# Seven products for every feature pair of both feed-forwards, with two of them made early on one token half, and 24 modulation columns moved into the mixing

## The chip, the cores and the metric

One core of a Trainium2 chip runs the whole program. The metric is device time in microseconds; lower is better. The kernel before takes 2085.41 us, the median of three runs (2083.35 to 2086.26).

## The reference

One layer over 1024 latent tokens and 256 context tokens of width 1024: feed-forward, token mixing, feed-forward, each behind a norm that is modulated by vectors computed from a condition, and a last norm.

```python
m_l = jnp.split(cond_lat @ ada_w[i] + ada_b[i], N_MOD, axis=-1)
x = x + 0.5 * m_l[2][:, None, :] * swiglu(modulate(rms_norm(x, norm1_w[i]), m_l[0], m_l[1]),
                                            ffn1_w1[i], ffn1_w3[i], ffn1_w2[i])
...
x = x + m_l[5][:, None, :] * y_l
x = x + 0.5 * m_l[8][:, None, :] * swiglu(modulate(rms_norm(x, norm3_w[i]), m_l[6], m_l[7]),
                                            ffn2_w1[i], ffn2_w3[i], ffn2_w2[i])
...
def swiglu(h, w1, w3, w2):
    return (jax.nn.silu(h @ w1) * (h @ w3)) @ w2
```

The context goes through the first feed-forward and the mixing with the same weights. `w1` and `w3` are 1024 x 2816, that is 22 features of 128 columns. The nine modulation vectors (0 to 8) have 8 columns of 128 numbers each.

## The kernel before, in words

Tensors lie with features on the partitions, tokens on the free axis, in two token halves of 512 (`tg` 0 and 1). Each f32 factor is split into a high and a low part (`hi` by a copy on ScalarE, `lo` by a subtraction on VectorE), and each product is three matmuls, hi hi, hi lo and lo hi (`mm3`, L426 to L428). A weight of one feature is 128 x 1024, loaded as two raw halves of 128 x 512 (`raw_half`, L659, a ring of NR = 6 tiles) and split into a ring of NH = 6 pairs (`half`, L666). All DMA goes through SyncE's (SP's) queue, in order.

**The hidden layer.** The classic way for two features is 2 features x 2 token halves x 8 blocks of 128 inputs, three matmuls each. `chain` (L699) does two features f and f + 1 in seven products instead, a scheme of Strassen's kind: `seven_w` (L679) makes seven combinations of the four quarters of the two weights (w1 to w7; w1 is the first half a11 of feature f, w2 its second half a12), and each is multiplied by a combination of four blocks of the input: b11 and b21 are the two halves of the inputs on token half 0, b22 the second on token half 1, and t1 to t4 are differences (the T blocks, made by `t_make`, L1101, or by `norm_t`, L633, and `t34_raw`). Each of the seven is four blocks deep, 12 matmuls. Sums of products are copied out of PSUM by ScalarE (`keep`), added by VectorE (`plus`) or accumulated in PSUM. `c_silu` and `c_mul` (L741) make silu(h w1) (h w3), and `g_out` (L749) makes the combinations of it that the back half uses and stores them in DRAM (`gd`). `hidden` (L816) runs `chain` for w1 and w3 of every pair, with `w2_sums` (L785) and some modulation columns (`mods`, up to MPER sums a call) between.

**The starts.** `chain` needs both token halves and the T blocks. So that TensorE has work before, features 0 to 3 of the first feed-forward and 0 and 1 of the second are done the classic way: `first1` (L1167) runs six weights of token half 0 block by block while the norm and its modulation columns are computed and token half 1 is loaded; `first2` (L1145) does the four weights of features 0 and 1 for token half 0, then 1. A dependency by hand (HELD) puts the last norm's diagonal matmuls (`rstd_rows`) behind the first seven blocks of `first2`.

**The columns.** A modulation column is one reduction on VectorE of 128 x 1024 products (`mod_sum`, L519; in halves of 512 in `mods_half`, L528). Ten come from small matmuls in `first1`, the others are spread over the first feed-forward (vectors 5, 2, 1, 0, 4, 3, 7, 6 in the order of EMODS), vector 8 over the second.

**Order.** `first1` is written in the order in which TensorE, VectorE and ScalarE run it. The feed-forwards are ordered by a scheduler that takes priorities from the program's order; loads and splits of weights are raised by 150 (WPRI). From the end of the first feed-forward to the start of the second a `Recorder` (L166) collects all operations, plans them with costs per engine and fixes the order of every engine; nearly all its instructions have the line L147. The mixing's tiles of 128 x 512 (`t`) come from a ring of NT2 = 5.

The first feed-forward's hidden layer runs to about 440 us, its back half and the context's to 850, the mixing to 1433, the second feed-forward to the end.

## Time and profile before

| | us |
|---|---|
| median of three runs | 2085.41 |
| the profiled execution | 2088.82 |
| its span, first to last instruction | 2087.0 |
| TensorE busy | 2071.6 (99%) |
| VectorE busy | 1471.9 (71%) |
| ScalarE busy | 973.3 (47%) |
| GpSimd busy | 199.3 (10%) |

The granted TensorE clock is 0.998 over the span, and the DMA engines moved 178 GB/s on average. On a page, `psa<-hh,whi` is a matmul that writes the PSUM tile psa from the moving operand hh and the weight whi; `x14` is a count; what stands in brackets behind a row of the timeline is the idle time before it and who ended it. PEld is the load of the stationary operand, which overlaps the matmuls.

### The profile page before, as it was taken

To read this page: it belongs to the slowest core of one execution; us is meant where nothing else is said; L and a number is where in the kernel's file an instruction comes from. 1 tells how busy PE (TensorE), PEld (TensorE's weight loads), DVE (VectorE), ACT (ScalarE), POOL (GpSimd) and SP (SyncE) were. 2 spreads that over 40 slices of the span, in tenths; PEclk is the share of its full clock that TensorE was granted. 3 is DMA by queue.
4 is the path that set the end of the run, shared out by engine and by line. 5 is a ranking of instruction groups with operands and counts; after the bars stand their busy time and mean duration, and the time that the engine had idled before them with its cause. 6 is when DMAs were issued, how large, how long until landed. Compare 5 with 4: busy or idle time off the path is not lost.

```text
span 2087.0 us, 34162 instructions
## 1 busy us (share of the span) xinstructions
PE 2071.6 (99%) x12352; PEld 1763.0 (84%) x12352; DVE 1471.9 (71%) x2660; ACT 973.3 (47%) x1818; POOL 199.3 (10%) x195
## 2 busy tenths in 40 slices
PE   9999999999999999999999999999999999999998
PEld 6888888888889999998788988888888888888888
DVE  6889999666776445765577478767776666765586
ACT  5433433435544445566475246444434344344553
POOL 0000000000015665001021001000000000010000
PEclk9999999999999999999999999999999999999999
DMA  9277667449886553674233233242344444477774
GB/s 348 84 241 237 232 217 256 149 165 371 277 289 222 181 183 115 195 219 129 76 108 98 79 91 105 90 162 81 112 156 147 144 163 157 151 235 229 218 237 151
DMA packets 201082, 370.58 MB, mean 178 GB/s; under 512 B 23249, under 2 KB 35921, under 8 KB 200785
## 3 DMA queue, kind: packets, MB, share of 16 engines
q1 hardware_dynamic: 200768, 368.33, 53.7%
q8 instruction: 97, 1.59, 0.3%
q14 instruction: 73, 0.59, 0.1%
q10 hardware_dynamic: 144, 0.07, 0.0%
HBM read 292.68 MB, written 67.24 MB: 172 GB/s over the span
## 4 chain that ended last, share of the span: by engine, by line
PE 77%; DVE 10%; DMA 8%; issue 3%; ACT 1%; SPq 0%; DVEq 0%; POOLq 0%; ACTq 0%
PE psa L147 18%; PE psa L426 10%; PE psa L428 10%; PE psa L427 10%; PE psb L147 9%; PE psb L427 7%; PE psb L428 7%; PE psb L426 7%; DVE junk L523 2%; DVE wlo L422 2%; DMA raw<-in_w 2%; DMA raw<-sd 2%; DVE hl L422 1%; DMA raw<-gd 1%; DMA hl<-sd 1%
## 5 line engine op out<-in xcount | busy, mean ns | idle before, releaser
L421 ACT ACTIVATE whi<-raw 128x512 fp32r<-128x512 f32 x371 | 233.9, 631 | 502.7 <-issue 160.6
L422 DVE TENSOR_TENSOR wlo<-raw,whi 128x512 fp32r<-128x512 f32 x371 | 254.1, 687 | 178.0 <-ACT whi L421 175.6
L426 PE MATMUL psa<-hh,whi 128*128 128x512 f32 x684 | 267.0, 390 | 1.2 <-ACT s L738 0.6
L428 PE MATMUL psa<-hh,wlo 128*128 128x512 f32 x684 | 266.3, 389 | 0.0
L427 PE MATMUL psa<-hl,whi 128*128 128x512 f32 x684 | 266.2, 389 | 0.0
L427 PE MATMUL psb<-hl,whi 128*128 128x512 f32 x568 | 221.6, 390 | 0.5 <-DVE hl L422 0.3
L428 PE MATMUL psb<-hh,wlo 128*128 128x512 f32 x568 | 221.3, 390 | 0.2 <-DVE wlo L422 0.2
L426 PE MATMUL psb<-hh,whi 128*128 128x512 f32 x568 | 221.1, 389 | 0.0
L426 PEld LDWEIGHTS psa<-hh,whi 128*128 128x128 f32 x684 | 128.4, 188 | 28.9 <-ACT s L711 1.7
L147 DVE TENSOR_TENSOR wlo<-raw,whi 128x512 fp32r<-128x512 f32 (+1 forms) x140 | 88.5, 647 | 90.8 <-ACT whi L147 80.1
L147 PE MATMUL psa<-hl,whi 128*128 128x512 f32 x384 | 152.5, 397 | 0.0
L147 PE MATMUL psa<-hh,whi 128*128 128x512 f32 x384 | 152.3, 397 | 0.0
L147 PE MATMUL psa<-hh,wlo 128*128 128x512 f32 x384 | 152.2, 396 | 0.0
L428 PEld LDWEIGHTS psa<-hh,wlo 128*128 128x128 f32 x684 | 128.4, 188 | 26.6
L427 PEld LDWEIGHTS psa<-hl,whi 128*128 128x128 f32 x684 | 128.5, 188 | 26.3
L422 POOL TENSOR_TENSOR hl<-s,hh 128x512 fp32r<-128x512 f32 x88 | 132.4, 1530 | 145.2 <-DVE hl L422 81.1
L147 ACT ACTIVATE whi<-raw 128x512 fp32r<-128x512 f32 (+1 forms) x140 | 82.5, 599 | 119.7 <-PE psa L147 94.1
L427 PEld LDWEIGHTS psb<-hl,whi 128*128 128x128 f32 x568 | 106.6, 188 | 24.7 <-DVE hl L422 2.7
L428 PEld LDWEIGHTS psb<-hh,wlo 128*128 128x128 f32 x568 | 106.6, 188 | 23.1 <-DVE wlo L422 1.2
L426 PEld LDWEIGHTS psb<-hh,whi 128*128 128x128 f32 x568 | 106.6, 188 | 22.2
L428 PE MATMUL psa<-hh,hl 128*128 128x256 f32 x392 | 111.1, 284 | 0.0
L426 PE MATMUL psa<-hh,hh 128*128 128x256 f32 x392 | 111.1, 283 | 0.0
(443 smaller groups left out, 4820.4 us busy)
## 6 DMA issues: line engine op xcount, KB each, us to landing
raw<-in_w SPq DMA_DIRECT2D x242, 256.0 KB, 3.3
s<-in_w SPq DMA_DIRECT2D x198, 256.0 KB, 3.7
gd<-s SPq DMA_DIRECT2D x154, 256.0 KB, 2.8
ada<-in_adaT SPq DMA_DIRECT2D x60, 512.0 KB, 4.6
raw<-gd SPq DMA_DIRECT2D x91, 256.0 KB, 3.5
sd<-s SPq DMA_DIRECT2D x44, 256.0 KB, 2.7
raw<-sd SPq DMA_DIRECT2D x44, 256.0 KB, 3.2
hh<-in_w SPq DMA_DIRECT2D x44, 256.0 KB, 4.0
```

Source lines behind the costliest of these rows:

```text
L147: self.rec.add(self.eng, lambda: f(*map(get, a), **{x: get(v) for x, v in k.items()}), outs, ins, name, a, k)
L421: nc.scalar.activation(hi, src, AF.Copy)
L422: (eng or nc.vector).tensor_tensor(out=lo, in0=src, in1=hi.bitcast(F32), op=ALU.subtract)
L426: mm(ps, wa[0], xa[0], start=start, stop=False, skip_group_check=more)
L427: mm(ps, wa[0], xa[1], start=False, stop=False, skip_group_check=more)
L428: return mm(ps, wa[1], xa[0], start=False, stop=stop, skip_group_check=more)
L523: nc.vector.tensor_tensor_reduce(out=self.junk, in0=t, in1=self.cs[s], scale=1.0, scalar=self.col("ada_b")[:, j:j + 1], op0=ALU.mult, op1= ...
```

## The change

Every pair of features now goes by seven products.

- For 8 of the 11 pairs of the first feed-forward (PARTS and the four that `first1` takes) and 6 of the second (PARTS2), the products w1 b11 and w2 b21 are done ahead: they need the even feature and token half 0 alone. `first1` and `parts` multiply the first four blocks, copy the partial sum c1 out (`c1_keep`) and store it in DRAM (`c1d`), add the other four blocks in PSUM, and go on through `c_silu` and `c_mul` to the gated product of the even feature, token half 0, which `g_part` stores in `gd`.
- `rest` does the other five products of such a pair: it loads c1 back through the ring of raw weights, copies it into a PSUM bank on ScalarE, and accumulates the third product on it. It loads the even feature's weights again, and the stored gated product for `g_out`.
- `first2` is gone; the classic products of token half 1 are gone from the first feed-forward. The T blocks are made in steps between the products of `parts`. Token half 1 in normalised form is only kept for the blocks 4 to 7 in the first feed-forward.
- The diagonal matmuls of the second feed-forward's opening are put behind four blocks instead of seven.
- The columns of vectors 5, 7 and 6 are taken out of the first feed-forward and reduced in halves in the mixing (`mods_mix`), three halves after each step of SEQ; in the first feed-forward a call of `mods` takes 2 sums beside `rest` and 5 beside `chain`.

TensorE's order at the opening of the second feed-forward, before. `nacc` are the squares of token half 1, `ndiag` its diagonals; the rows with hh and hl are the first product:

```order
L427 MATMUL psa_15857<-hl_3072_15484,whi_15821 128x512
L147 MATMUL psb_15690<-ones_83,nacc_15403 128x1 x4
L428 MATMUL psa_15857<-hh_3071_15473,wlo_15822 128x512
L426 MATMUL psa_15857<-hh_3073_15480,whi_15821 128x512
L427 MATMUL psa_15857<-hl_3074_15491,whi_15821 128x512
L428 MATMUL psa_15857<-hh_3073_15480,wlo_15822 128x512
L426 MATMUL psa_15857<-hh_3075_15507,whi_15821 128x512
L427 MATMUL psa_15857<-hl_3076_15518,whi_15821 128x512
L428 MATMUL psa_15857<-hh_3075_15507,wlo_15822 128x512
L147 MATMUL psb_15706<-ndiag_15698,ones_83 128x128
```

The first row is the 14th matmul of the feed-forward; seven lie between the sums and the diagonals. The same place in TensorE's order after:

```order
L427 MATMUL psa_16038<-hh_3185_15719,whi_16016 128x512
L147 MATMUL psb_15943<-ones_83,nacc_15656 128x1 x4
L428 MATMUL psa_16038<-hl_3186_15730,whi_16016 128x512
L429 MATMUL psa_16038<-hh_3185_15719,wlo_16017 128x512
L427 MATMUL psa_16090<-hh_3179_15677,whi_16028 128x512
L428 MATMUL psa_16090<-hl_3180_15691,whi_16028 128x512
L147 MATMUL psb_15959<-ndiag_15951,ones_83 128x128
```

The first row is the 10th matmul, and four lie between the sums and the first diagonal.

SP's queue during `first1`, before (`ada` are modulation columns, `x` the blocks of token half 1):

```order
L476 DMA ada_128_464<-in_adaN 128x1024
L1362 DMA x_129_466<-in_xT 128x512
L1362 DMA x_130_468<-in_xT 128x512
L1362 DMA x_131_470<-in_xT 128x512
L513 DMA ada_133_511<-in_adaT 128x1024
L476 DMA ada_134_513<-in_adaN 128x1024
L1362 DMA x_135_515<-in_xT 128x512
```

And after:

```order
L1472 DMA x_123_462<-in_xT 128x512
L764 DMA c1d<-s_467 128x512
L764 DMA c1d<-s_486 128x512
L764 DMA c1d<-s_492 128x512
L764 DMA c1d<-s_506 128x512
L764 DMA c1d<-s_512 128x512
L764 DMA c1d<-s_518 128x512
L514 DMA ada_131_521<-in_adaT 128x1024
L477 DMA ada_132_523<-in_adaN 128x1024
L1472 DMA x_133_525<-in_xT 128x512
```

The six stores of partial sums, each of which waits for its copy on ScalarE, now stand between the third block of x and the last columns.

The diff, cut to what the steps below speak of:

```diff
+    def mods_mix(self, pool):
+        nc = self.nc
+        for o in (0, 512):
+            row = self.tile(self.cp2, [P, 512], F32, "wgr")
+            nc.sync.dma_start(row, self.I["c"][:, o:o + 512].broadcast_to([P, 512]))
+            nc.scalar.activation(row, row, AF.Silu)
+            for j in [8 * m + k for m in MMODS for k in range(KD)]:
+                m = self.mod[0][:, j:j + 1]
+                t = self.t2(pool)
+                nc.sync.dma_start(t, self.I["adaT"][j][:, o:o + 512])
+                nc.vector.tensor_tensor_reduce(out=t, in0=t, in1=row, scale=1.0, scalar=m if o else self.col("ada_b")[:, j:j + 1],
+                                               op0=ALU.mult, op1=ALU.add, accum_out=m)
+                if o and j % 8 == 7:
+                    self.mod_fin(j, 0)
+                yield
...
+    def prod4(self, wh, b, ps, start, stop=True):
+        return [self.mm3(ps, [t[:, k * P:(k + 1) * P] for t in wh], b[k], start and k == 0, k == 3, not start) for k in range(4)]
+
+    def g_part(self, f):
+        self.nc.sync.dma_start(self.gd[1, f // 2], self.g[f, 0])
+        self.g[f, 0] = None
+
+    def c1_keep(self, f, i, ps):
+        t = self.stile()
+        self.nc.scalar.copy(t, ps)
+        self.nc.sync.dma_start(self.c1d[i, f // 2], t)
+
+    def parts(self, fs, steps, first=None):
+        groups = [fs[i:i + 2] for i in range(0, len(fs), 2)]
+        order = [(f, i, q) for g in groups for q in range(2) for f in g for i in range(2)]
+        todo, ready, ps = deque(order), deque(), {}
+
+        def ahead():
+            if todo:
+                f, i, q = todo.popleft()
+                ready.append(self.load_half((self.w1, self.w3)[i][f][:, 512 * q:512 * q + 512]))
+
+        ahead(), ahead(), ahead()
+        yield
+        for f, i, q in order:
+            ahead()
+            if not q:
+                ps[f, i] = (self.psB if i else self.psA)()
+            mms = self.prod4(ready.popleft(), self.h[0][4 * q:4 * q + 4], ps[f, i], not q)
+            if first:
+                first(mms)
+                first = None
+            if not q:
+                self.c1_keep(f, i, ps[f, i])
+            elif not i:
+                self.c_silu(f, 0, ps[f, i], True)
+            else:
+                self.c_mul(f, 0, ps[f, i])
+                self.g_part(f)
+            if i:
+                next(steps, None)
+
+    def five_w(self, w, f):
+        e = self.nc.vector
+        lo, hi = slice(0, 512), slice(512, 1024)
+        a11, a21, a22 = (self.raw_half(w[i][:, q]) for i, q in ((f, lo), (f + 1, lo), (f + 1, hi)))
+        s1 = self.raw_half()
+        a12 = self.raw_half(w[f][:, hi])
+        e.tensor_tensor(out=s1, in0=a21, in1=a22, op=ALU.add)
+        e.tensor_tensor(out=a21, in0=a11, in1=a21, op=ALU.subtract)
+        e.tensor_tensor(out=a11, in0=s1, in1=a11, op=ALU.subtract)
+        r = [self.half(a11), self.half(s1), self.half(a21)]
+        e.tensor_tensor(out=a12, in0=a12, in1=a11, op=ALU.subtract)
+        return r + [self.half(a12), self.half(a22)]
+
+    def rest(self, w, f, out, bank):
+        nc, i = self.nc, int(w is self.w3)
+        with self.tc.high_priority(offset=WPRI):
+            c1 = self.raw_half(self.c1d[i, f // 2])
+            w6, w5, w7, w3, w4 = self.five_w(w, f)
+        t1, t2, t3, t4 = self.T
+
+        def keep(ps):
+            t = self.stile()
+            nc.scalar.copy(t, ps)
+            return t
+
+        def plus(o, x, y):
+            nc.vector.tensor_tensor(out=o, in0=x, in1=y, op=ALU.add)
+            return o
+
+        a, b = bank(), bank()
+        nc.scalar.copy(a, c1)
+        self.prod4(w6, t2, a, False)
+        u2 = keep(a)
+        self.prod4(w5, t1, b, True)
+        c5 = keep(b)
+        self.prod4(w7, t3, a, False)
+        u3 = keep(a)
+        out(f + 1, 1, plus(c5, u3, c5))
+        if i:
+            self.g[f, 0] = self.stile()
+            nc.sync.dma_start(self.g[f, 0], self.gd[1, f // 2])
+            self.again.add(f)
+        self.prod4(w3, self.h[1][4:], b, False)
+        out(f, 1, plus(u2, b, u2))
+        self.prod4(w4, t4, a, False)
+        out(f + 1, 0, a, True)
+
...
-        put(1, b11), put(2, b21), put(3, b22)
+        if f not in self.again:
+            put(1, b11)
+        put(2, b21), put(3, b22)
...
-    def hidden(self, f0, mods=lambda: None, hold=False):
+    def hidden(self, f0, mods=lambda: None, hold=False, parts=0):
         for f in range(f0, NF, 2):
             if hold and f == NF - 2:
                 self.held = []
-            self.chain(self.w1, f, self.c_silu, self.psA)
+            chain = self.rest if f < parts else self.chain
+            chain(self.w1, f, self.c_silu, self.psA)
             if f > f0:
-                mods()
-            self.w2_sums(f // 2 - 1)
-            self.chain(self.w3, f, self.c_mul, self.psB)
+                mods(*MPER[f >= parts:][:1])
+            if f:
+                self.w2_sums(f // 2 - 1)
+            chain(self.w3, f, self.c_mul, self.psB)
             if f > f0:
-                mods()
+                mods(*MPER[f >= parts:][:1])
...
-    def first2(self, tp, diag):
-        t3 = [self.tile(tp, [P, 512], F32R, f"t3l{k}") for k in range(4)]
-        t3 = [tuple(t3[2 * i:2 * i + 2]) for i in range(2)]
-        ws = {}
-        for f in range(2):
-            for i, w in ((0, self.w1), (1, self.w3)):
-                ws[f, i] = self.load_halves(w[f], t3 if (f, i) == (1, 1) else (None, None))
-        for tg in LATTG:
-            for f in range(2):
-                ps = self.psA()
-                mms = self.proj(ws[f, 0], tg, ps)
-                if tg == f == 0:
-                    self.tc.add_manual_dep(diag.ins, mms[HELD].ins.name, SCHED, reason="order")
...
-            raws[i, q] = self.raw_half((self.w1, self.w3)[i % 2][i // 2][:, 512 * q:512 * q + 512])
+            raws[i, q] = self.raw_half((self.w1, self.w3)[i % 2][i // 2 * 2][:, 512 * q:512 * q + 512])
...
                 mms(i, st, (0, 2, 1))
+                if st == 3:
+                    self.c1_keep(i // 2 * 2, i % 2, pss[i])
...
-        self.c_mul(1, 0, pss[3])
-        self.c_silu(2, 0, pss[4], True)
-        ps = self.psA()
-        for k in range(KD):
-            if k == 2:
-                pr = self.rstd_rows(r, 512, n1, dg=dg)
-            self.mm3(ps, self.wslice(ws[6], k), self.h[0][k], k == 0, k == KD - 1)
-        rb[1] = self.scr(n1, "nrb")
-        nc.scalar.copy(rb[1], pr)
-        norm_a = lambda k: self.norm_a(1, k, a, b, rb[1], n1, self.x[1][k])
-        norm_a(0)
...
-        self.c_mul(3, 0, self.H(ws[7], 0))
-        return ws
+        self.c_mul(2, 0, pss[3])
+        self.g_part(2)
+        self.c_silu(4, 0, pss[4], True)
+        ps = [self.psA(), self.psA()]
+        for i in range(2):
+            for k in range(4):
+                if i == 0 and k == 2:
+                    pr = self.rstd_rows(r, 512, n1, dg=dg)
+                self.mm3(ps[i], self.wslice(ws[6 + i], k), self.h[0][k], k == 0, k == 3)
+            if i == 0:
+                rb[1] = self.scr(n1, "nrb")
+                nc.scalar.copy(rb[1], pr)
+                norm = lambda k: self.norm_a1(1, k, a, rb[1], self.x[1][k])
+                norm(4)
+            self.c1_keep(6, i, ps[i])
+            if i == 0:
+                self.norm_a2(1, 4, b, self.x[1][4])
+        self.prod4(ws[6][1], self.h[0][4:], ps[0], False)
+        self.prod4(ws[7][1], self.h[0][4:], ps[1], False)
+        run = self.parts(PARTS, self.t_steps)
+        for k in (4, 5, 6, 7):
+            if k < 7:
+                norm(k + 1)
+                self.norm_a2(1, k + 1, b, self.x[1][k + 1])
+            if k == 4:
+                self.c_mul(4, 0, pss[5])
+                self.g_part(4)
+                self.norm_b(1, k, b, self.x[1][k])
+                next(run)
+            else:
+                self.norm_b(1, k, b, self.x[1][k])
+            if k == 6:
+                self.c_silu(6, 0, ps[0], True)
+        for k in range(4):
+            norm(k)
+        self.c_mul(6, 0, ps[1])
+        self.g_part(6)
+        return run
...
+        cols = self.mods_mix(pool)
         for s in SEQ:
             eval(s, {**globals(), **locals()})
+            for _ in range(MMPER):
+                next(cols, None)
+        for _ in cols:
+            pass
...
-            ws = self.first1((xp, xp, None), n1)
+            box = []
+            self.t_steps = (x for g in box for x in g)
+            run = self.first1((xp, xp, None), n1)
             cls("n1"), cls("f1w")
             self.tp = tp = opn("tp")
-            t_steps = self.t_make(xp, tp)
-            for f in range(4):
-                self.c_silu(f, 1, self.H(ws[2 * f], 1), True)
-                next(t_steps)
-                self.c_mul(f, 1, self.H(ws[2 * f + 1], 1))
-                if f % 2:
-                    next(t_steps)
+            box.append(self.t_make(xp, tp))
+            for _ in run:
+                pass
+            for _ in self.t_steps:
+                pass
...
+        def t_steps():
+            for i, raw in enumerate((self.t1r, self.tr)):
+                for k in range(4):
+                    self.t_split(tp, i, k, raw[k])
+                    if k % 2:
+                        yield
+            raw = []
             for k in range(4):
-                self.t_split(tp, i, k, raw[k])
-        raw = self.first2(tp, rec.diags[-4])
+                raw.append(self.t34_raw(k))
+                if k % 2:
+                    yield
+            for k in range(4):
+                self.t3_split(k, raw[k][0])
+            yield
+            for k in range(4):
+                self.t4_split(k, raw[k][1])
+
+        hold = lambda mms: tc.add_manual_dep(rec.diags[-4].ins, mms[3].ins.name, SCHED, reason="order")
+        steps = t_steps()
+        for g in (self.parts(PARTS2, steps, hold), steps):
+            for _ in g:
+                pass
         late = (None for _ in self.mods_half(f2, (8,)))
-        for k in range(4):
-            self.t3_split(k, raw[k][0])
-        for k in range(4):
-            self.t4_split(k, raw[k][1])
-        self.hidden(2, lambda: next(late, None))
+        self.hidden(0, lambda n: next(late, None), False, 2 * len(PARTS2))
...
-        self.hidden(4, lambda: mods(MPER), True)
+        self.hidden(0, mods, True, 8 + 2 * len(PARTS))
...
-HELD = 6
-EMODS = ((5, (0,)), (2, (0, 1)), (1, (1,)), (0, (1,)), (4, (0, 1)), (3, (0, 1)), (7, (0,)), (6, (0,)))
-MPER = 6
+PARTS2 = (0, 2, 4, 6, 8, 10)
+EMODS = ((2, (0, 1)), (1, (1,)), (0, (1,)), (4, (0, 1)), (3, (0, 1)))
+MMPER = 3
+MMODS = (5, 7, 6)
+MPER = (2, 5)
+PARTS = (8, 10, 12, 14)
```

33 lines of the change are left out of this document (12 added, 21 removed).

## The prediction

> **What bounds the kernel now.** I read the page first, then the busy times by stage, then TensorE's waits.
>
> ```profile
> PE 2071.6 (99%) x12352; PEld 1763.0 (84%) x12352; DVE 1471.9 (71%) x2660; ACT 973.3 (47%) x1818; POOL 199.3 (10%) x195
> ...
> 150.00:390.00 240.00, 239.17 (x1046) 195.25 (x1045) 230.26 (x383) 90.87 (x161) 0.00 (x0) 1.00 0.70 230
> 390.00:450.00 60.00, 60.00 (x266) 49.67 (x266) 36.24 (x57) 26.68 (x47) 0.00 (x0) 1.00 0.41 138
> 860.00:1430.00 570.00, 567.25 (x4676) 488.49 (x4676) 385.03 (x860) 300.56 (x600) 51.40 (x84) 1.00 0.40 120
> 1430.00:1505.00 75.00, 74.41 (x335) 61.13 (x334) 62.56 (x104) 34.26 (x58) 1.01 (x1) 1.00 0.24 78
> 1505.00:1885.00 380.00, 380.00 (x1678) 314.76 (x1677) 254.19 (x413) 149.35 (x260) 5.58 (x8) 1.00 0.50 167
> ...
> PE psb L147 <- issue: 1.9, 2, 1.6
> ```
>
> Columns of the stage rows: window, its length, then busy time (and instructions) of PE, PEld, DVE, ACT and POOL, granted clock, DMA share, GB/s. TensorE is busy in 99% of the span and its longest wait is 1.9 us in total, so the kernel is one long queue of matmuls and the time is their number times their spacing. Busy time hides small stalls, because a matmul's record overlaps the next one; the count shows them. In 390 to 450 us there are 4.43 matmuls per us, in 150 to 390 only 4.36: 18 fewer than the faster rate would give, while DVE there is busy in 230.26 of 240 us. So the first feed-forward has a DVE-bound stretch, worth a few us, and everywhere else matmuls bound.
>
> ```profile
> 91.25 0.39 PE L426 MATMUL psa<-hh,whi 128*128 128x512 f32 x1
> ...
> 92.16 0.39 PE L427 MATMUL psa<-hl,whi 128*128 128x512 f32 x1
> ```
>
> A record lasts 0.39 us, but four starts lie in 0.91 us: the spacing is 0.2267 us (the count 266 in 60 us gives 0.226). The spacing, not the 0.39, is what a matmul costs.
>
> **Term 1: the matmuls removed.** A pair of features and one weight costs 96 matmuls in the classic form (2 features x 2 token halves x 8 blocks x 3) and 7 x 12 = 84 in the seven-product form. Before, two pairs of the first feed-forward and one of the second are classic, with two weights each: 3 x 2 x 12 = 72 matmuls more than if all were seven-product. After, every pair is: 24 matmuls in `parts` or `first1` (the products w1 and w2 of the seven, which only need the even feature and token half 0) and 60 in `rest`. The order of TensorE's instructions has 72 fewer 128x512 matmuls, all else equal, so that the change does what it says is no open question. 72 x 0.2267 = **16.3 us less**.
>
> **Term 2: VectorE in the first feed-forward.**
>
> ```profile
> 1457.44 0.68 DVE L422 TENSOR_TENSOR t1l<-t2h,t1h 128x512 fp32r<-128x512 f32 x1
> 1458.04 0.68 DVE L422 TENSOR_TENSOR t1l<-t2l,t1h 128x512 fp32r<-128x512 f32 x1
> ...
> L523 DVE CUSTOM_DVE_ANT_0 junk<-ada,condc,cols 128x1024 bf16<-128x1024 f32 x54 | 68.9, 1277 | 6.0 <-DMA ada<-in_adaT 4.1 <-ACT condc L455 1.7
> ```
>
> Back to back a 128x512 operation takes 0.60 us of VectorE, a modulation column 1.28. A pair of `chain` before: 2 x (7 splits + 4 sums of weights + 3 sums of products) + 4 products with the gate + 4 in `g_out` + 2 in `w2_sums` = 38 operations, with 12 columns 22.9 + 15.4 = 38.3 us, against 168 x 0.2267 = 38.1 us of matmuls: just saturated, as the stage row shows. A pair of `rest` after: 2 x (5 + 4 + 2) + 3 + 4 + 2 = 31 operations and 4 columns, 18.7 + 5.1 = 23.8 us against 120 x 0.2267 = 27.2 (88%); the three last pairs, with 10 columns, 35.8 against 38.1 (94%). The matmuls that the stretch lost come back: between 0.8 us (its idle time on TensorE) and 18 x 0.2267 = 4.1. I take **2.0 us less**, nearer the idle time, since records can be missing.
>
> ```profile
> L421 ACT ACTIVATE whi<-raw 128x512 fp32r<-128x512 f32 x371 | 233.9, 631 | 502.7 <-issue 160.6
> ...
> L711 ACT COPY s<-psa 128x512 f32<-128x512 f32 x76 | 42.8, 570 | 0.0
> ```
>
> In `rest` ScalarE makes 10 splits, 2 copies of c1 into PSUM, 6 copies out and 3 silu per pair, 21 x about 0.6 = 12.6 of 27.2 us; the matmuls hide them. The new wait there is the copy of c1 for its load. Behind it stand the copies that free TensorE's banks, but the load is issued as soon as the copy of the `rest` before has left its slot, some 13 us earlier. DMA per pair of `rest`: 10 loads for the two weights, 1 of g, 6 stores of g, 5 for the sums of w2, 22 x 256 KB, and two or three columns of 512 KB, 7 MB in 27.2 us or about 260 GB/s.
>
> ```profile
> 500.00:550.00 50.00, 50.00 (x226) 41.56 (x225) 34.80 (x62) 25.94 (x50) 0.69 (x1) 1.00 0.87 303
> ...
> DMA to landing us min/median/max: 2.5/3.5/7.2
> ```
>
> The back half already runs at 303 GB/s with TensorE at its full rate (226 in 50 us). The second line is the landing time of the raw weights in 150 to 390 us, for the rival below.
>
> **Term 3: the start.** After the fourth block, `first1` copies six partial sums out and puts six stores of 256 KB on SP's queue, ahead of the load of the last modulation columns, five blocks of x and the next weights.
>
> ```profile
> 40.52 0.33 SPq L476 DMA_DIRECT2D ada<-in_adaN  x1
> 40.90 2.57 SPq L1362 DMA_DIRECT2D x<-in_xT  x5
> ...
> 35.00:40.00 5.00, 5.00 (x37) 3.81 (x36) 4.08 (x8) 2.30 (x5) 0.00 (x0) 1.00 0.92 294
> 40.00:45.00 5.00, 5.00 (x37) 3.76 (x36) 3.68 (x8) 2.82 (x6) 0.00 (x0) 1.00 0.95 351
> 45.00:50.00 5.00, 4.94 (x35) 3.34 (x33) 3.67 (x7) 2.03 (x4) 0.00 (x0) 1.00 1.04 386
> ...
> 49.44 0.64 PE L482 MATMUL psb<-ada,ccol 128*32 128x128 f32 x16
> ...
> ada<-in_adaN SPq DMA_DIRECT2D x2, 512.0 KB, 5.0
> ```
>
> The DMA engines are full here (0.92 to 1.04), so 6 x 262 KB = 1.57 MB of stores push what follows by 1.57/0.37 = 4.2 us, at the 351 to 386 GB/s of these rows. The columns issued at 40.52 land 5.0 us later, at 45.5, and are read at 49.44: 3.9 us of slack, 0.3 too little. The x blocks and weights behind (40.90 and later) are pushed as far, but `first1` needs its second weights later than before. The six copies on ScalarE lie in its gaps; it is busy 2.3 of 5 us. Bounds 0 and 4.2 us; I take **0.5 us more**, near the difference of slack and push.
>
> **Term 4: the opening of the second feed-forward.** TensorE starts on token half 0 while half 1 is still being normalised; then come the column sums of half 1 (`nacc`) and the four diagonals (`ndiag`).
>
> ```profile
> 1432.81 0.39 PE L426 MATMUL psa<-hh,whi 128*128 128x512 f32 x1
> ...
> 1436.03 1.05 PE L147 MATMUL psb<-ones,nacc 128*128 128x1 f32 x8
> 1436.94 0.48 PE L428 MATMUL psa<-hh,wlo 128*128 128x512 f32 x1
> ...
> 1438.75 1.16 PE L147 MATMUL psb<-ndiag,ones 128*128 128x128 f32 x8
> ...
> 1456.53 0.39 PE L428 MATMUL psa<-hh,t3l 128*128 128x512 f32 x1
> 1457.52 0.50 PE L426 MATMUL psa<-hh,whi 128*128 128x512 f32 x1 [0.59 <-ACT s L738]
> ```
>
> Before, 14 matmuls (3.2 us) lie ahead of the sums and 7 between their end and the diagonals (1436.94 to 1438.75, 1.8 us), and both find their operands all but ready. The order after has 10 (2.3 us) and 4 (0.9 us). What VectorE, GpSimd and ScalarE do meanwhile is unchanged, so TensorE waits 3.2 - 2.3 = 0.9 us for the sums and 1.8 - 0.9 = 0.9 us for the diagonals, **1.8 us more**. Behind the waiting matmul stand only matmuls. The stall at 1457.52 (0.99 - 0.23 = 0.76 us, token half 1 late) goes, because half 1 is first needed after 288 matmuls (65 us): **0.8 us less**; the 56 VectorE operations that make half 1 and the T blocks (0.6 to 0.7 each) have 65 us instead of 192 x 0.2267 = 44.
>
> **Term 5: 24 columns in the mixing.**
>
> ```profile
> L538 DVE CUSTOM_DVE_ANT_0 s<-s,row,mod 128x512 f32<-128x512 f32 x8 | 6.0, 745 | 0.3 <-DMA s<-in_adaT 0.3
> L147 ACT ACT_TABLE_LOAD x10 | 12.8, 1283 | 0.2
> ...
> 1022.64 0.33 PE L147 MATMUL psb<-zq,zk 128*32 128x32 f32 x16 [0.21 <-DVE zk L147]
> 1024.60 0.33 PE L147 MATMUL psb<-zq,zk 128*32 128x32 f32 x16 [1.63 <-issue]
> ...
> 1025.60 0.63 PE L147 MATMUL psb<-p89T,wg 128*128 128x512 f32 x1
> 1026.03 0.63 PE L147 MATMUL psa<-hl,whi 128*128 128x512 f32 x1
> ...
> 1000.00:1050.00 50.00, 48.04 (x615) 39.35 (x615) 30.04 (x70) 23.79 (x55) 1.02 (x1) 0.97 0.23 68
> ```
>
> 48 halves of columns at 0.745 us are 35.8 us of VectorE in a stage where it is busy 385 of 570 us: 74% instead of 68%, and TensorE is busy 567. Two table loads of 1.28 us come to ScalarE, and 50 loads of 256 KB to a DMA that is 0.40 busy. A reduction that waits for its load holds VectorE, with the GLA chain's `AB` operations behind it, for which TensorE waits at 1024.60. If nothing waits it costs nothing; if TensorE waits through each, 35.8 us. The recorder re-plans the stage. It changes between the two kinds of matmul 209 times instead of 185; a return costs (1436.94 above: 0.48 instead of 0.39) 0.09 us, so 12 more visits cost 1.1 us and a little at entry. Gone, at best, are the 2.75 us idle and the half clock after 1024.60 (starts 0.43 us apart; 0.03 x 50 = 1.5 us). Bounds -4 and +35.8; I take **1.5 us more**, near the end where TensorE's row is full.
>
> **The sum**: -16.3 - 2.0 + 0.5 + 1.8 - 0.8 + 1.5 = -15.3 us. The profiled execution took 2088.8 us (span 2087.0), so 2073.5; the median of the runs is 3.4 us lower, 2085.4, which gives **2070 us**.
>
> **Rivals.** (a) *The new waits cost more than themselves.* The row at 1024.60 shows TensorE idle for 1.63 us and then half clock; two waits of 0.9 us in term 4, or a re-planned chain in the mixing without matmuls between, would each lose some 1.5 us more, and the start 3: 2070 + 1.5 + 1.5 + 3 = 2076. For it: full DMA at the start. Against: the stall of 0.76 us at 1457 left the spacing as it was. The Trainium skill, "TensorE: Matmul & The Clock Gate", section "What's actually happening", has the clock halved only after about 3.4 us of idle window; by that rule term 4 stays at 1.8 us, by the row it is 3.3. The trace's gap of 1.63 us speaks against the rule being that lenient.
>
> (b) *The mixing goes VectorE-bound at places*: if half of the 48 reductions delay TensorE by 0.745 us each, 18 us, all gains are gone: 2088. Against: 185 us of idle VectorE.
>
> (c) *Slower: the ring of raw weights.* `rest` takes six tiles of a ring of six, c1 among them, where `chain` took five. So a tile is loaded into the slot that the same tile of the `rest` before leaves when it is split; the last of them, a22, is split after the fourth product of the one before that (10.9 us into it, and 1.3 for the split). Load 3.5, three sums and a split 3.1: 18.8 us, and TensorE needs it at 2 x 13.6 = 27.2, so 8.4 us of slack. Landings over 11.9 us would make TensorE wait; the longest seen is 7.2. It decides at 0.55 us per `rest` (28 of them take back 15.3); at 1 us each it ends at 2070 + 28 = 2098.
>
> **Chances**: forecast (2063 to 2076) 0.68; (a) 0.12; (b) 0.11, half of it still under 2081; (c) and other losses past 2090 0.09. The range 2062 to 2083 holds about 8 in 10 and stops short of (c). A measurement of this kernel tells 0.2% (4.2 us) from no change; faster by more than that 0.82, within it 0.08, slower 0.10.
>
> **What would show it.** Right: matmul rate above 4.4 per us in all of the first feed-forward, VectorE under 95% there; two waits near 0.9 us ahead of `nacc` and `ndiag` at the opening, none at token half 1; no new wait over 1 us in the mixing. Wrong: waits of TensorE for `wlo` or for c1's copy in each `rest` (c); for `zk`, `AB` in the mixing (b); a wait for `ada` or the first weights before 70 us (a).

## The result: 0.65% slower, and the profile after

The changed kernel takes 2098.17 us (median of 4 runs, 2096.21 to 2100.46) against 2084.92 for the kernel before: a ratio of 1.0065, 95% interval 1.0052 to 1.0077. The forecast was 2070. The time is the 2098 of the third rival, but that it meets it so closely is chance: of the 28 us over the forecast, the runs below tie only 16.5 to the rival's ring of tiles.

First the page's busy times, then the stages of the prediction in the changed kernel (columns as there).

```profile
PE 2064.5 (99%) x12280; PEld 1750.6 (84%) x12280; DVE 1485.7 (71%) x2732; ACT 1004.2 (48%) x1884; POOL 208.6 (10%) x195
```

```profile
150.00:390.00 240.00, 233.80 (x1011) 191.16 (x1011) 206.30 (x341) 95.89 (x172) 0.00 (x0) 0.99 0.69 231
390.00:450.00 60.00, 60.00 (x267) 49.69 (x265) 38.20 (x61) 24.35 (x43) 0.00 (x0) 1.00 0.42 142
860.00:1430.00 570.00, 568.69 (x4687) 488.35 (x4686) 416.76 (x963) 305.00 (x608) 54.51 (x84) 1.00 0.46 145
1430.00:1505.00 75.00, 72.21 (x324) 58.98 (x323) 59.15 (x97) 39.27 (x69) 1.01 (x1) 1.00 0.47 154
1505.00:1885.00 380.00, 375.51 (x1640) 306.37 (x1639) 256.06 (x419) 151.72 (x268) 5.61 (x8) 1.00 0.55 183
```

The 72 matmuls are gone (12352 to 12280), yet TensorE's rate fell: 1011 matmuls in 150 to 390 us, where it should have risen from 1046, and 1640 in the second hidden layer, where it should have stayed at 1678. TensorE's waits say for whom:

```profile
PE psb L427 <- ACT s L818: 7.9, 7, 2.4
PE psb L427 <- ACT whi L422: 3.2, 1, 3.2
PE psb L429 <- DVE wlo L423: 2.5, 4, 1.1
PE psa L427 <- ACT s L763: 2.1, 1, 2.1
```

These are new: the copies out of PSUM in `rest` (L818), a weight's split in `parts` (L422), and the copy of a partial sum, c1 (L763). The wait for wlo was there before, with 0.2 us. By stage, from the starts of the same instructions in each trace (hidden: from the first matmul behind `first1`'s six weights, or of the second feed-forward, to the first sum of its back half, whose first matmuls it so includes):

| us | start | hidden 1 | back half 1 and context | mixing | hidden 2 |
|---|---|---|---|---|---|
| before | 58.9 | 460.4 | 346.4 | 567.1 | 491.6 |
| after | 61.2 | 465.7 | 345.3 | 565.2 | 495.5 |
| after, as forecast | 59.4 | 447.5 | 346.4 | 568.6 | 487.2 |

The losses against the forecast: 18 us in the first hidden layer, 8 in the second, 1.8 at the start; the mixing did 3.4 better and the back half 1.1. That makes the 24 us between the profiled execution (2097.56) and the 2073.5 that was forecast for it; the 28 of the medians is more mainly because the profiled execution of the kernel before lay 3.4 above its median.

**How one wait comes about.** The first hidden layer at 258 us: TensorE, ScalarE, SyncE's queue and VectorE of the changed kernel (in the queue, the time of a row runs from its first issue to its last; in brackets, the idle time before a row).

```profile
258.64 0.39 PE L429 MATMUL psa<-x,wlo 128*128 128x512 f32 x1
261.48 0.50 PE L427 MATMUL psb<-x,whi 128*128 128x512 f32 x1 [2.45 <-ACT s L818]
```

```profile
255.21 0.64 ACT L422 ACTIVATE whi<-raw 128x512 fp32r<-128x512 f32 x1 [3.65 <-DVE raw L804]
255.75 0.63 ACT L845 ACTIVATE s<-s 128x512 f32<-128x512 f32 x1
258.28 0.59 ACT L826 COPY psb<-raw 128x512 f32<-128x512 f32 x1 [1.89 <-DMA raw<-c1d]
...
260.86 1.06 ACT L818 COPY s<-psb 128x512 f32<-128x512 f32 x2
```

```profile
249.83 3.84 SPq L514 DMA_DIRECT2D ada<-in_adaT  x2
254.54 0.33 SPq L681 DMA_DIRECT2D raw<-c1d  x1
```

```profile
249.95 1.28 DVE L524 CUSTOM_DVE_ANT_0 junk<-ada,condc,cols 128x1024 bf16<-128x1024 f32 x1
...
252.02 1.28 DVE L524 CUSTOM_DVE_ANT_0 junk<-ada,ada,cols 128x1024 bf16<-128x1024 f32 x1
...
253.83 0.69 DVE L423 TENSOR_TENSOR wlo<-raw,whi 128x512 fp32r<-128x512 f32 x1
```

Read from the bottom: column reductions stand on VectorE between the splits. The split at 253.83 frees a tile of the raw ring, and only then, at 254.54, is c1's load issued. It lands at 258.28; ScalarE had waited 1.89 us for it, with the copies that empty TensorE's banks queued behind (260.86), and TensorE starts at 261.48. The queue had also stood 2.5 us at the second column's load, for a tile that a reduction held, but the wait for the split ended last.

It is so in most of the 16 `rest` of this hidden layer: in 13 the wait of c1's load ends with a split on VectorE, and c1 lands at a median of 0.02 us before ScalarE copies it. ScalarE's waits for it, between 61 and 450 us:

```profile
ACT psb L826 <- DMA raw<-c1d: 7.6, 7, 1.9
ACT psa L826 <- DMA raw<-c1d: 5.1, 3, 2.6
```

VectorE, from 135 to 335 us:

```profile
L423 DVE TENSOR_TENSOR wlo<-raw,whi 128x512 fp32r<-128x512 f32 x70 | 47.4, 684 | 3.8 <-ACT whi L422 3.7
L524 DVE CUSTOM_DVE_ANT_0 junk<-ada,ada,cols 128x1024 bf16<-128x1024 f32 x25 | 31.9, 1278 | 0.1
L524 DVE CUSTOM_DVE_ANT_0 junk<-ada,condc,cols 128x1024 bf16<-128x1024 f32 x19 | 24.3, 1279 | 0.1
```

These are VectorE's largest groups there, in a stretch in which seven pairs of `rest` run: 25 + 19 = 44 columns, 6.3 a pair. Ten more lie in `parts`, between 81 and 132 us, and the last of the 54 starts at 311 us: none is left beside the three `chain` pairs. The text of the program asks for 4 a pair beside `rest`; the scheduler took the others forward.

### The profile page after: what moved, and what is told of

Its sections match the earlier page's. It is cut to its first block, busy times and chain, and to the rows that moved or that the text cites. A ratio compares the mean times of both kernels' runs of the same rounds, so it can differ in the third digit from the quotient of the medians.

```text
span 2095.8 us, 34463 instructions
## 1 busy us (share of the span) xinstructions
PE 2064.5 (99%) x12280; PEld 1750.6 (84%) x12280; DVE 1485.7 (71%) x2732; ACT 1004.2 (48%) x1884; POOL 208.6 (10%) x195
## 5 line engine op out<-in xcount | busy, mean ns | idle before, releaser
L422 ACT ACTIVATE whi<-raw 128x512 fp32r<-128x512 f32 x391 | 244.4, 630 | 475.9 <-issue 113.2
L423 DVE TENSOR_TENSOR wlo<-raw,whi 128x512 fp32r<-128x512 f32 x391 | 266.4, 687 | 180.7 <-ACT whi L422 175.5
L427 PE MATMUL psa<-hh,whi 128*128 128x512 f32 x628 | 244.8, 390 | 2.1 <-ACT s L763 2.1
L428 PE MATMUL psa<-hl,whi 128*128 128x512 f32 x628 | 244.5, 389 | 0.0
L429 PE MATMUL psa<-hh,wlo 128*128 128x512 f32 x628 | 244.4, 389 | 0.0
L427 PE MATMUL psb<-hh,whi 128*128 128x512 f32 x584 | 228.1, 391 | 3.8 <-ACT whi L422 3.2
L429 PE MATMUL psb<-hh,wlo 128*128 128x512 f32 x584 | 228.4, 391 | 2.2 <-DVE wlo L423 2.2
L147 PE MATMUL psa<-hh,whi 128*128 128x512 f32 x384 | 152.3, 397 | 0.0
L147 PE MATMUL psa<-hl,whi 128*128 128x512 f32 x384 | 152.1, 396 | 0.0
L147 PE MATMUL psa<-hh,wlo 128*128 128x512 f32 x384 | 152.1, 396 | 0.0
L427 PEld LDWEIGHTS psa<-hh,whi 128*128 128x128 f32 x628 | 118.0, 188 | 27.1 <-ACT s L763 2.6
L429 PEld LDWEIGHTS psa<-hh,wlo 128*128 128x128 f32 x628 | 117.9, 188 | 24.4
L428 PEld LDWEIGHTS psa<-hl,whi 128*128 128x128 f32 x628 | 117.9, 188 | 24.1
```

The source lines that it names most:

```text
L147: self.rec.add(self.eng, lambda: f(*map(get, a), **{x: get(v) for x, v in k.items()}), outs, ins, name, a, k)
L422: nc.scalar.activation(hi, src, AF.Copy)
L423: (eng or nc.vector).tensor_tensor(out=lo, in0=src, in1=hi.bitcast(F32), op=ALU.subtract)
L427: mm(ps, wa[0], xa[0], start=start, stop=False, skip_group_check=more)
L428: mm(ps, wa[0], xa[1], start=False, stop=False, skip_group_check=more)
L429: return mm(ps, wa[1], xa[0], start=False, stop=stop, skip_group_check=more)
```

## The experiments

Theories: **1**, the columns' loads in SyncE's queue; **2**, the ring, the forecast's slower rival; **3** (formed after the first two groups of runs), VectorE full with hoisted columns; **4**, hand-set or planned places on ScalarE, for what remained. Each ratio is to the kernel before, run beside it (medians 2084.9 to 2086.4).

| run | median us | ratio (95%) |
|---|---|---|
| mixing alone | 2085.52 | 0.9998 (0.9989 to 1.0007) |
| first feed-forward and mixing | 2092.31 | 1.0029 (1.0020 to 1.0038) |
| second feed-forward alone | 2087.14 | 1.0007 (0.9998 to 1.0016) |
| no columns | 2080.12 | 0.9972 (0.9960 to 0.9985) |
| reductions without loads | 2087.21 | 1.0002 (0.9991 to 1.0013) |
| loads without reductions | 2082.99 | 0.9980 (0.9970 to 0.9989) |
| column loads on another queue | 2099.40 | 1.0064 (1.0049 to 1.0079) |
| c1 in a tile of s | 2320.11 | 1.1127 (1.1110 to 1.1143) |
| columns pinned | 2086.02 | 0.9999 (0.9989 to 1.0008) |
| c1's own ring | 2081.68 | 0.9980 (0.9971 to 0.9989) |
| pinned, vector 8 in the mixing | 2085.38 | 0.9998 (0.9989 to 1.0008) |
| that and c1's own ring | 2081.80 | 0.9977 (0.9968 to 0.9987) |
| c1's own ring, T1 batched | 2079.67 | 0.9972 (0.9963 to 0.9981) |
| that, copies first | 2075.03 | 0.9960 (0.9946 to 0.9974) |
| that, pinned | 2072.77 | 0.9943 (0.9931 to 0.9955) |
| that, stores on another queue | 2073.95 | 0.9948 (0.9936 to 0.9960) |

### Which part of the change

The kernel before with `mods_mix` and the shorter EMODS alone:

> The kernel before with one part of the change: the 24 columns of vectors 5, 7 and 6 reduced in halves in the mixing, both feed-forwards as before. Reading of the traces so far: the mixing (from its first matmul at 865.7 or 872.0 us to the first matmul of the second feed-forward) lasted 567.1 us before and 565.2 after, and the first feed-forward loses 24 of its columns, 24 x 1.28 = 31 us of VectorE in the stretch where VectorE was full. So 0 to 4 us from the feed-forward and 2 us from the mixing: 2079 to 2083 us. Rival (the columns hold VectorE in the mixing, as in the second rival of the prediction): 2086 to 2100.

No change (2085.5 against 2085.4). Its mixing lasts 565.6 us: the 24 columns cost nothing there, and the second rival is dead. The expected gain of the hidden layer is seen in the stage (458.1 instead of 460.4) but not in the total: the second hidden layer, the same program, took 493.6 instead of 491.6 in this execution. Such differences of 2 us between executions limit what a stage can tell.

The changed kernel with the old `first2` opening and `chain` in the second feed-forward:

> The changed kernel with the second feed-forward as before (its first pair classic, the other ten by chain, the norm of its token half 1 as before). By the stages of the two traces, the first feed-forward's back half starts 7.4 us later and the mixing gains 1.9 (with the context's part 1.2 more): 2085 + 4.3 = 2089 us. If the loss were made mostly at the second feed-forward's opening instead: 2075 to 2080.

The kernel before with only the new second feed-forward:

> The kernel before with the second feed-forward of the changed kernel and nothing else. By the stages of the two traces, the second feed-forward's hidden layer lasts 3.9 us longer and the end 0.4: 2085 + 4.3 = 2089 us. If that stage's loss came only from what the first feed-forward or the mixing left behind (an order of the planner, say): 2085 - 5.4 = 2080.

The first feed-forward with the mixing loses 7 us (0.29%) instead of gaining 11, the second 1.8 (not told from none) instead of gaining 4.4. Both halves miss, the first by far the most; 7.0 + 1.8 is also less than the 13.2 of the whole.

### Columns: loads or reductions

Without the columns beside the hidden layers:

```diff
-                    self.mod_col(*todo.pop())
+                    self.no_col(*todo.pop())   # memset of one number per partition
```

> The changed kernel without the modulation columns beside the hidden layers: those that the hidden layer of the first feed-forward holds and the 8 of the second are neither loaded nor reduced, each is set to a constant by a tiny operation; nothing else is left out. Theory 1 (the queue): the columns' loads, 512 KB each on SyncE's one queue in order, and their reductions on VectorE and the operations in order behind them make c1 and the weights late, and TensorE waits: nearly all of the 25 us of new waits go, 2098 - 22 = 2076 us or below, with TensorE's waits in the first hidden layer under 3 us. Theory 2 (the ring: c1 is the sixth tile of a ring of six, so every load of rest comes too late whatever else stands in the queue): the waits on the copies behind c1 stay, 2090 us or more.

18 of the 28 us between result and forecast came back. This is what full rate looks like, 884 matmuls in 200 us, beside the changed kernel in the same window:

```profile
135.00:335.00 200.00, 200.00 (x884) 165.41 (x883) 141.32 (x224) 86.89 (x154) 0.00 (x0) 1.00 0.61 204
```

```profile
135.00:335.00 200.00, 193.26 (x831) 157.26 (x830) 185.37 (x309) 80.67 (x145) 0.00 (x0) 0.98 0.76 252
```

53 matmuls are missing after, 12 us. The run speaks for theory 1 against 2 as they were worded; the following runs divide it. It doesn't clear the ring: c1's load still waits for a split in 15 of 16 `rest`, with VectorE busy in only 141 of 200 us, and c1 lands a median of 0.5 us before its copy. ScalarE's waits for it are down to 1.5 us. The column reduced from a resident tile:

```diff
-                    self.mod_col(*todo.pop())
+                    j, ctxs = todo.pop()
+                    self.mod_sum(j, self.cs[0], ctxs)
```

> The changed kernel with the columns beside the hidden layers (all of the first feed-forward's hidden layer and the 8 of the second) reduced from a tile that is already resident: the reductions stay on VectorE with their full length, the 512 KB or 256 KB loads are left out. Without both, the run before took 2080. Theory 1a (the loads in SyncE's queue and in the DMA engines make c1 and the weights late, and a reduction that waits for its load holds VectorE): near 2080, 2077 to 2084. Theory 1b (VectorE's busy time: 1.28 us of a reduction between the splits that TensorE waits for): near 2098, 2092 to 2100.

The column loaded, and one element of it copied:

```diff
-            nc.vector.tensor_tensor_reduce(out=self.junk, in0=t, in1=self.cs[s], ...
+            nc.vector.tensor_copy(self.mod[s][:, j:j + 1], t[:, s:s + 1])
```

> The changed kernel with the same columns loaded but not reduced: an operation of one element per partition reads each tile and puts a wrong number into the modulation, so the reductions themselves, 1.28 us each, are left out while VectorE still waits for each load and the tile comes free as early as it can. Theory 1a (loads): 2090 to 2098, with TensorE's waits on c1's copy still there. Theory 1b (busy time of VectorE, which also holds the column tiles and so SyncE's queue): 2078 to 2084.

Leaving out the loads brings back 11 us, leaving out the reductions 15, both 18 (13, 18 and 19 by the ratios, which allow for the different sessions): neither theory 1a nor 1b is right alone, and VectorE's time is the larger part. The loads from GpSimd's queue:

```diff
-        self.nc.sync.dma_start(t, self.I["adaT"][j])
+        (self.nc.gpsimd if len(self.cs) > 1 else self.nc.sync).dma_start(t, self.I["adaT"][j])
```

> The changed kernel, all work kept, with the loads of those columns issued from GpSimd's queue instead of SyncE's: bytes, reductions and their order on VectorE stay, but a column load that waits for a free tile no longer holds the loads of c1 and of the weights behind it. If the queue's order is the place (theory 1a by the queue): most of the 18 us come back, 2080 to 2086. If it is the bytes on the DMA engines or VectorE's time: 2093 to 2100.

No gain in all: a column's place ahead of c1 in SyncE's queue isn't the cause of the whole. By stage, the first hidden layer got longer (470.8 us) and the second shorter (489.8). In the second one, a late column held VectorE in the changed kernel, and a sum of weights behind it, for whose split TensorE then waited 1.3 us:

```profile
1607.10 0.75 DVE L539 CUSTOM_DVE_ANT_0 s<-s,row,cols 128x512 f32<-128x512 f32 x1 [3.25 <-DMA s<-in_adaT]
1607.78 0.09 DVE L539 DVE_READ_ACCUMULATOR2_ANT mod<- 128x1 f32 x1
1607.81 0.69 DVE L806 TENSOR_TENSOR raw<-raw,raw 128x512 f32<-128x512 f32 x1
```

### The ring

c1 in a tile of the ring of 19:

```diff
-            c1 = self.raw_half(self.c1d[i, f // 2])
+            c1 = self.stile()
+            nc.sync.dma_start(c1, self.c1d[i, f // 2])
```

> The changed kernel with c1 loaded into a tile of the ring of 19 (s) instead of the ring of six raw weights; nothing else changes. Theory 2 (the ring of six for six tiles, the slower rival of the prediction): 2078 to 2086, the waits of TensorE on the copies behind c1 gone. Theory 1 (queue and columns): at most the part of the waits where c1 waited for a slot, 2092 to 2098.

222 us slower, which no theory expected. TensorE waits for c1's copy into PSUM in nearly every `rest`, up to 11.4 us:

```profile
PE psa L427 <- ACT psa L827: 110.0, 14, 11.4
PE psb L427 <- ACT psb L827: 66.6, 13, 7.1
```

By the trace c1's load waits for no tile now. It stands in SyncE's order behind stores of `g_out` that wait for VectorE, a column's load or loads for the sums of w2, is issued later still, and ScalarE waits up to 9.7 us for it; why the scheduler put it there isn't shown. It is no test of the ring, but shows the lever: the time at which c1's load is issued. So c1 got two tiles that nothing else uses, with two fewer in the ring of 19:

```diff
-            c1 = self.raw_half(self.c1d[i, f // 2])
+            c1 = self.tile(self.fp, [P, 512], F32, "c1", 2)
+            nc.sync.dma_start(c1, self.c1d[i, f // 2])
-NS = 19
+NS = 17
```

> The changed kernel with c1 loaded into two tiles of its own (the ring s has 17 instead of 19 for it), so that rest takes five tiles of the ring of six, as chain does, and c1 can come a rest earlier. Theory 2 (the ring, the prediction's slower rival): 2080 to 2088, TensorE's waits on the copies behind c1's load gone. Theory 3 (VectorE full with hoisted columns): the waits move to the splits of the weights, 2092 to 2099.

16.5 us below the changed kernel, as theory 2 said. In the first hidden layer c1 now lands 11.6 us or more before its copy, and ScalarE never waits for it. Whether a seventh tile in the ring would have done the same was not tried. Theory 3's other half was tried beside it: each reduction tied, in the scheduler's order alone, behind the last matmul before its call.

```diff
+            self.pin = self.last
...
+            if self.pin:
+                self.tc.add_manual_dep(r.ins, self.pin.ins.name, SCHED, reason="order")
```

> The changed kernel, all work kept; each column reduction of the first hidden layer is tied, in the scheduler's order alone, behind the last matmul of the rest or chain after which the program's text asks for it. In the changed kernel's order of VectorE, 7 columns stand in parts and 45 between the first and the last rest (up to 7 a pair), one beside the chain pairs; pinned, it is none in parts, 4 a pair beside rest and 26 beside the three chain pairs. Theory 3 (the scheduler hoists columns into rest and parts; VectorE is then busy 185 of 200 us there, 26.8 us a pair against 27.2 of matmuls, instead of the 23.8 that the prediction counted, and what it waits for is no longer made up): the first hidden layer shortens from 465.7 to 455 us, the time is 2085 to 2090. Theory 2 (the ring) or a loss from the bytes alone: within 4 of 2098.

12 us below, as theory 3 said. ScalarE's waits for c1 are 1.2 us instead of 12.7. The trace has no column in `parts` now, 26 between 135 and 335 us and 28 behind. The same window of the two runs, c1's own ring first, then pinned:

```profile
135.00:335.00 200.00, 199.16 (x878) 164.20 (x877) 189.44 (x315) 85.66 (x153) 0.00 (x0) 1.00 0.75 256
```

```profile
135.00:335.00 200.00, 199.67 (x881) 165.03 (x880) 169.43 (x277) 87.34 (x155) 0.00 (x0) 1.00 0.72 243
```

With c1's own ring VectorE is busier than ever (189 of 200 us, 43 columns) and TensorE at its rate; pinned, c1 is in the ring, VectorE has 30 us to spare, and TensorE is at its rate too. But that execution, 2079.49 us, is the fastest of the ten with pinned columns, whose median is 2086.02; what the others lose isn't seen in it. Then vector 8 was moved to the mixing on top of the pinning, and last all three were put together:

```diff
-MMODS = (5, 7, 6)
+MMODS = (5, 7, 6, 8)
-        late = (None for _ in self.mods_half(f2, (8,)))
+        late = iter(())
```

> The pinned kernel with the 8 columns of vector 8 taken out of the second feed-forward too and reduced in the mixing with the 24 others, so that no late column load can hold VectorE there. Theory 3 with its second half (in the second feed-forward a reduction waits 3.25 us for its late load and the split that TensorE needs stands behind it): 5 us below the pinned kernel. If those waits have another cause: the same as the pinned kernel, within 2.

> All three edits together: columns pinned, vector 8 in the mixing, c1 in two tiles of its own. Sum of the parts by theory 3 with a little from the ring: 2077 to 2083, below the kernel before. If only the ring mattered, as much as c1's own ring alone.

Vector 8 in the mixing shortens the second hidden layer by 4.5 us in the trace (490.8 to 486.3) and lengthens the mixing by 3.6 (565.6 to 569.2): no change in all. With c1's own ring as well, the second hidden layer is not shorter (490.7 against 490.1 with the ring alone), so even these differences may be those of single executions. With all three the time is that of c1's own ring alone, 2081.8, which is what was expected if only the ring mattered, though the sum of the parts (2077 to 2083) covers it too. So the two causes **are not equal**. With tiles of its own for c1, the hoisted columns cost nothing that the total shows (2081.7 with them, 2081.8 when they are pinned and vector 8 is moved). With c1 in the ring, they cost 12 us, and some 4 us of loss stay when they are pinned (2086.0 against 2081.7, and 2085.4 against 2081.8). The ring with no tile to spare is the condition; the full VectorE makes most of the loss out of it. What the remaining 4 us are isn't shown.

### What remained

From 2081.7 to the forecast some 12 us were missing. In `parts`, ScalarE and VectorE of the changed kernel pass four blocks to and fro, 2.4 us each, with a weight's split behind them in the written order:

```profile
84.12 0.63 ACT L422 ACTIVATE t1h<-x 128x512 fp32r<-128x512 f32 x1 [1.77 <-DVE x L1230]
86.59 0.63 ACT L422 ACTIVATE t1h<-x 128x512 fp32r<-128x512 f32 x1 [1.84 <-DVE x L1230]
88.94 0.63 ACT L422 ACTIVATE t1h<-x 128x512 fp32r<-128x512 f32 x1 [1.72 <-DVE x L1230]
89.48 0.61 ACT L422 ACTIVATE whi<-raw 128x512 fp32r<-128x512 f32 x1
```

```diff
         for k in range(4):
             tt(out=x1[k], in0=x1[k], in1=x0[k], op=ALU.subtract)
+        for k in range(4):
             self.split(x1[k], *one[k])
```

> c1 in its own ring, and the first step of the T blocks written as four subtractions and then four splits instead of block by block. In every run so far VectorE and ScalarE pass each of the four blocks to and fro in 2.0 us, 8 us in all, and the split of a weight stands behind them in ScalarE's written order, for which TensorE waits 2.7 to 3.4 us at 86 us and then runs at half clock for some 7 matmuls. Theory 4 (this order is what parts loses): the wait at 86 us goes, the time is 4 us below the one with c1's own ring, 2077 to 2079. If the weight's load is late anyway (it is issued behind stores that wait): the wait stays within 1 us, 2081 to 2083.

The wait at 86 us is gone; the four splits run in one row:

```profile
82.77 2.44 ACT L422 ACTIVATE t1h<-x 128x512 fp32r<-128x512 f32 x4 [0.88 <-DVE x L1231]
85.11 0.61 ACT L422 ACTIVATE whi<-raw 128x512 fp32r<-128x512 f32 x1
```

The gain is 2 us, half of what was expected, and not told from none: the intervals overlap. (The wait that went was 1.1 to 4.3 us long in the traces before, not 2.7 to 3.4.) The first hidden layer is only 1.0 us shorter in the trace: with VectorE busy in 190 of the 200 us from 135, TensorE has 867 matmuls there instead of 878. In the second feed-forward of the changed kernel the first copies of c1 stand behind T splits that nothing needs yet:

```profile
1462.33 0.63 ACT L422 ACTIVATE t2h<-t3h 128x512 fp32r<-128x512 f32 x1
1462.86 0.61 ACT L422 ACTIVATE whi<-raw 128x512 fp32r<-128x512 f32 x1
1463.38 0.61 ACT L422 ACTIVATE t2h<-t3h 128x512 fp32r<-128x512 f32 x1
1463.90 0.57 ACT L763 COPY s<-psa 128x512 f32<-128x512 f32 x1
```

```diff
+                    r = self.t_split(tp, i, k, raw[k])
+                    tc.add_manual_dep(r.ins, self.kept.ins.name, SCHED, reason="order")
```

> The run before it, and in the second feed-forward the splits of the first T blocks are ordered behind the copy of the last partial sum made, so that ScalarE's copies out of PSUM come before eight splits that nothing needs for 60 us. Theory 4: TensorE's wait of 2.3 us for the first copy (at the second half of the first product, 18 us into the second feed-forward) goes: 2 to 2.5 us below the run before it. If the copies wait for something else than their place in the order: no change, within 1.

4.6 us less, and the wait on the first copy is gone. Expected were 2 to 2.5; the second hidden layer is 4.0 us shorter in the trace (492.0 to 488.0). Half clock explains the surplus there: in the run before, it follows this wait of 2.2 us, and a granted clock of 0.81 over 9 us is another 1.7. The run before, then this one:

```profile
1449.00:1458.00 9.00, 6.83 (x23) 5.12 (x23) 6.45 (x11) 5.99 (x11) 0.00 (x0) 0.81 0.61 203
```

```profile
1449.00:1458.00 9.00, 9.00 (x41) 7.47 (x40) 7.86 (x14) 8.94 (x18) 0.00 (x0) 1.00 0.88 305
```

> The run before it with the columns pinned to their places beside rest and chain. By the square of runs the pinning is worth nothing more once c1 has its own ring: within 1.5 of the run before it. If VectorE's hoisted columns still cost by themselves: 2 to 4 us below it.

2.3 us less, 0.17%: in the range of the second expectation by its size, but the intervals overlap, so it isn't told from nothing. In the trace TensorE has 884 matmuls between 135 and 335 us, where the run before has 872.

> The run before it with the stores of c1 in the first feed-forward issued from GpSimd's queue instead of SyncE's. If the six stores hold the columns and blocks of x behind them in SyncE's order while each waits for its copy: the first matmul comes at 59 instead of 61 us, and the time is 2 us lower. If their bytes or the new order in the written start are what costs: no change, within 1.

No change: the columns are issued at 41.05 us, close to the 40.52 before the change, but TensorE's first matmul behind `first1` comes at 61.0 all the same. The order in SyncE's queue isn't what the start loses.

The best version, with c1's own ring, the T1 blocks batched, the copies first and the columns pinned, takes 2072.77 us, 0.57% less than the kernel before (0.45 to 0.69%). Its stages: start 61.0, hidden layers 449.1 and 485.8, mixing 564.6 us.

## Why the prediction was wrong

1. **Matmuls removed** (-16.3): right. The page counts 72 fewer, and with the waits cured the hidden layers last 449.1 and 485.8 us, where the forecast's terms give 447.5 and 487.2.
2. **VectorE in the first feed-forward** (-2.0, measured about +16): this step failed, in two places, and is the main error. "A pair of `rest` after: ... 31 operations and 4 columns, 18.7 + 5.1 = 23.8 us ... (88%)" took the columns from the program's text. The trace has 6.3 a pair, and 185.4 us over seven pairs are 26.5 us, 97% of 27.2. And "the load is issued as soon as the copy of the `rest` before has left its slot, some 13 us earlier" is not what happens at 258 us: the load waits for a split on VectorE and is issued 3.7 us ahead of its landing, with nothing to spare. The ring is the condition: with tiles of its own for c1 the hoisted columns do no harm that the total shows (2082 with and without them), with c1 in the ring they make 2098 out of 2086. In the kernel before VectorE was as full (230 of 240 us) without this loss: `chain` took five tiles of six and kept c1 on the chip.
3. **The start** (+0.5, measured +2.3): inside its bounds of 0 to 4.2, but mis-sized. The DMA engines are full there (shares of 0.90 to 1.03), and the load of the columns comes at 43.42 instead of 40.52 us. What the prediction looked at, the columns, makes TensorE wait 0.6 us. More comes from a block of x behind them in the queue, for which ScalarE waits 2.6 us before it squares it, with the last reduction of `first1` behind that in VectorE's order (52.56 instead of 50.26 us); TensorE then waits 1.1 us for the normalised block:

```profile
50.50 1.31 ACT L590 ACTIVATE nsq<-x 128x512 f32<-128x512 f32 x2 [2.56 <-DMA x<-in_xT]
```

The run with the stores on another queue gave nothing back, so the order isn't it; that the bytes make it is only argued.
4. **The opening of the second feed-forward** (+1.8 - 0.8): the wait for the diagonals came (0.6 us in the waits instead of 0.9), the one for the sums was 0.2 by the starts of the matmuls, and the old stall went. Missed was a wait of 2.1 us for the first copy of c1, on ScalarE behind the T splits; the prediction looked at TensorE's order there and not at ScalarE's. TensorE's other waits in the second feed-forward are 1.7 us for ScalarE's splits, 1.2 for the copies of `rest` and 0.9 for VectorE's splits.
5. **Columns in the mixing** (+1.5, measured -1.9 in the trace): right that no long wait came. The run with the mixing alone shows no cost in the total.

Rival (c) named the right resource and had the slack of 8.4 us wrong. It counts from the slot that the same tile of the `rest` before leaves; in the trace c1's load waits for a split, and even without columns, on a VectorE busy in 141 of 200 us, c1 lands a median of 0.5 us ahead of its copy. Why c1 gets such a slot isn't shown. With nothing to spare, each delay on the fuller VectorE became a wait. Rival (a) was right that waits cost more than themselves, though not at the places it named (at the opening of the second feed-forward the granted clock stayed at 1.00): each of three waits was followed by half clock. Below, two of them in the granted clock of their windows, then the matmuls behind the second wait:

```profile
86.00:98.00 12.00, 8.27 (x28) 6.00 (x28) 12.00 (x20) 7.29 (x14) 0.00 (x0) 0.86 0.62 207
171.00:178.00 7.00, 4.83 (x15) 3.55 (x14) 5.71 (x11) 3.12 (x6) 0.00 (x0) 0.76 0.82 267
```

```profile
173.92 0.79 PE L427 MATMUL psb<-x,whi 128*128 128x512 f32 x1 [2.17 <-ACT s L818]
174.51 0.63 PE L428 MATMUL psb<-x,whi 128*128 128x512 f32 x1
...
176.64 0.63 PE L427 MATMUL psb<-x,whi 128*128 128x512 f32 x1
177.07 0.46 PE L428 MATMUL psb<-x,whi 128*128 128x512 f32 x1
```

The starts lie 0.43 us apart, the first 0.59, for some 3 us: seven matmuls that lose 1.5 us, on top of a wait of 2.2. (By the granted clock, 0.76 over 7 us, it is 1.7.) The Trainium skill, "TensorE: Matmul & The Clock Gate", section "What's actually happening", asks for an idle window of about 3.4 us, which is longer than each of these waits (2.2, 2.4 and 3.2 us). By that rule none of the three would have cost more than itself; the trace decides against it.

## What to carry to other kernels

Count the work that a scheduler may move (low priority, ready early) from the planned order of the engine, not from the loops that ask for it; here the difference was 6.3 instead of 4 columns a pair, and VectorE busy in 93 instead of 85% of the 200 us. A slack computed from durations has to be checked against the planned order: which release the load waits for, and what stands ahead of that release on its engine. When a tile is brought back from memory, give its load a buffer of its own; in this ring of six tiles for six, it was loaded only when a split on VectorE let it.

## What the runs showed of the hardware

Half clock followed waits of TensorE of 2.2, 2.4 and 3.2 us amid dense matmuls in the changed kernel, but not one of 2.1 us at 1464 us. The length doesn't decide it: that wait, for the first copy of c1 in the second feed-forward, is 2.0 to 2.2 us long in eleven of the traces, and half clock follows it in five (without columns, columns from another queue, c1's own ring, all three edits, T1 batched) and not in six. Each time the granted clock lost 1.7 us in all, as 3.4 us at half would. Moving the column loads to GpSimd's queue (GpSimd is then busy 11.1 us between 135 and 335 us, 0 otherwise) neither sped up nor slowed the whole.
